# A planned kernel whose scheduler counts TensorE's turns between large and small products

## The chip, the cores and the metric

The kernel runs on one core of one Trainium2 chip. The metric is the device time of one execution in microseconds, the median of several runs. Before the change it is 1898.14 us (three runs, 1898.09 to 1899.59).

## The reference

The reference is a two-layer decoder trunk on one sequence of 1024 positions and 1024 channels, in float32. Each layer computes `x + rms_norm(mixer(rms_norm(x)))`.

- Layer 0 projects the normed input with one matrix into two groups. Group A is a gated DeltaNet of 8 heads (key and value width 128): a causal convolution of four taps and SiLU on q, k and v, then a recurrence over time, `S = exp(g) S (I - beta k k^T) + beta k v^T`, `o = S^T q`. Group B is an S5 recurrence: 64 groups of 16 channels with 64 complex states each, then GELU and a gate `y * sigmoid(y @ w_glu)`. Each group is multiplied by a SiLU gate, and both go through one output projection of 2048 by 1024.
- Layer 1 projects into four parts of 2048 channels (b, c, h, z), computes `b * conv3(c * h) * silu(z)` with a causal convolution of three taps, and projects back with a matrix of 2048 by 1024.

## The kernel before

The kernel does not issue its instructions in the order in which the code names them. Every engine call goes through a recorder (`Queue`, `Plan.record`, line 154): it notes the engine, the tiles read and written, a duration from a table (`Plan.cost`, line 170) and a priority. The priority is the place of the call in the program; inside `with nc.after(n)` (line 92) n is added, which makes the calls less urgent. When all is recorded, `Plan.order` (line 222) plays the program through: an instruction is ready when what it depends on has ended and its tiles have a buffer; each engine, when free, takes the ready instruction of lowest priority number; the time goes on by the table's duration. `Plan.emit` (line 318) then issues all instructions in the order of the planned start times, through one line, so that the whole profile stands under line 323. What the plan decides is thus the order on each of the queues (TensorE, VectorE, ScalarE, GpSimd, SyncE's DMAs); on the chip each queue runs in that order, and every instruction starts when its semaphores allow.

The precision of float32 comes from pairs. A factor is split into a high and a low part of the fp32r type (`split`, line 368: a ScalarE copy and a VectorE subtraction), and a product is three fp32r matmuls of 128x128 by 128x512: high by high, high by low, low by high. Matmuls that add into the same PSUM bank form a chain in the plan: the next is ready when the one before has ended. The small work stays in plain float32: transposes against an identity, products with 128 columns, and products on 32x32 and 64x64 tiles.

The work in order of the program:

- `setup` (line 532) loads x in 8 blocks of 128 rows, normalizes, and transposes into hh and hl (`to_hT`, tiles hTp).
- S5 runs in 8 rounds (`s5_front`, `s5_scan`, `s5_back`: tiles mbp, pk, px on TensorE, then py), between projections (`u_proj`, `z_proj`: tile mm).
- DeltaNet runs in a pipeline over heads (line 517 on): in one turn the front of head i-1, the back of head i-2, and the projections of head i, which stand under `nc.after(400)`. The front (line 1009) transposes k (ktp), multiplies k by k and q (kk), transposes v (pv) and q (qtp), and inverts a triangular matrix (`invert`, line 1118: tiles iy, it, ip, in levels of 32 and 64 with copies on VectorE and a long substitution on GpSimd). The back (line 1062) is a chain over 8 chunks (pks, pz, pS) and a transpose (po).
- `glu` (line 1175), then the first output projection (`out_proj`, line 1225): first all 8 row blocks for the lower half of the channels, then all 8 for the upper half. When the upper half of a row block is done, `finish` (line 1289) normalizes it: ScalarE squares, VectorE scales, GpSimd takes the power -1/2 (tiles orr and n1r). Then `to_B` (line 427), under `nc.after(150)`, transposes it in two groups of four (tile hTq, PSUM of the ring g, which has three banks), and ScalarE copies the result out (tile r). From block 4 on, GpSimd combines the copies (tiles Bx and r).
- Layer 1 (`layer1`, line 1355) multiplies 2x2 blocks by a scheme of seven products instead of eight (`proj2`, line 1303; products p1 to p7, shown as p). The first two need blocks 0 to 3 alone; the others need `combine` (line 469), which follows GpSimd's work on blocks 4 to 7, and sums of the weights (tiles s, wb, wa), also on GpSimd.
- The second output projection (`out_proj1`, line 1380) writes the result.

The table of durations for TensorE has, in us: fp32r with n columns n/2400 + 0.0134; a transpose n/1200 + 0.003; plain float32 with 128 stationary columns n/600 + 0.005; narrow tiles 0.03 to 0.115. A turn from one kind to another costs nothing in the plan.

Of the kernel before, what the change touches and what calls it, by code (L numbers as in the profile page):

```python
# [10 lines left out]
F32R = mybir.dt.float32r  # L11
# [48 lines left out]


class Op:
    __slots__ = ("eng", "call", "dur", "dma", "deps", "succ", "wait", "ready", "start", "tiles", "prio", "port")


class Queue:
# [7 lines left out]
class Plan:  # L74
# [4 lines left out]

    LAT = dict(PE=0.2, DVE=0.12, ACT=0.15, Pool=0.11)  # L80

    WINDOW = 3.4133

    def __init__(self, nc):
# [69 lines left out]
    def record(self, eng, call, method, a, k):  # L154
        op = Op()
        op.eng, op.call, op.deps, op.succ, op.prio = eng, (call, a, k), {}, [], len(self.ops) + self.prio
        isap = lambda x: isinstance(x, bass.AP)
        outs = [x for x in a[:1] if isap(x)] + [k[n] for n in ("out", "accum_out") if n in k]
        ins = [x for x in a[1:] if isap(x)] + [x for n, x in k.items() if n not in ("out", "accum_out") and isap(x)]
        for x in ins:  # L160
            self.touch(op, x, False)
        for x in outs:
            self.touch(op, x, True)
        op.dma = method == "dma_start"
        op.dur = self.cost(eng, method, outs, ins, a, k)
        op.port = self.port(op, ins, method)
        self.ops.append(op)


# [50 lines left out]
        return t.tag.rsplit("_", 2)[0]  # L220

    def order(self):
        from heapq import heappush, heappop
        ops = self.ops
        rings = {}
        for h in self.tiles.values():
            t = h["tile"]
            h["n"] = len(h["users"])
            if t.space != bass.MemoryType.DRAM:
                rings.setdefault(self.ring(t), []).append(h)  # L230
        for op in ops:
            op.tiles, op.wait, op.ready = [], len(op.deps), 0.0
            for j, kind in op.deps:
                ops[j].succ.append((op, kind))
        for h in self.tiles.values():
            for op in h["users"]:
                op.tiles.append(h)
                if h["tile"].space != bass.MemoryType.DRAM:
                    op.wait += 1
        idx = {op: i for i, op in enumerate(ops)}  # L240
        later = {e: [] for e in ("PE", "DVE", "ACT", "Pool", "SP")}
        now = {e: [] for e in later}
        free = {e: 0.0 for e in later}
        hw = dma = port = 0.0
        clock, edge, busy = 1.0, self.WINDOW, 0.0

        def unblock(op, t):
            op.ready = max(op.ready, t)
            op.wait -= 1
            if op.wait == 0:  # L250
                heappush(later[op.eng], (op.ready, op.prio, idx[op]))

        def grant(ring, t):
            h = ring.pop(0)
            for op in h["users"]:
                unblock(op, t)

        for op in ops:
            if op.wait == 0:
                heappush(later[op.eng], (0.0, op.prio, idx[op]))  # L260
        for key, hs in rings.items():
            for _ in range(min(self.caps.get(key, 1), len(hs))):
                grant(hs, 0.0)
        done = []
        while len(done) < len(ops):
            e = min(later, key=lambda e: free[e] if now[e] else max(free[e], later[e][0][0]) if later[e] else 1e18)
            t = free[e] if now[e] else max(free[e], later[e][0][0])
            while later[e] and later[e][0][0] <= t:
                r, p, i = heappop(later[e])
                heappush(now[e], (p, i))  # L270
            op = ops[heappop(now[e])[1]]
            op.start = t
            done.append(op)
            if op.dma:
                issue, move, late = op.dur
                if e == "Pool":
                    free[e] = t + issue
                    dma = max(dma, t + issue + 1.0) + move
                else:
                    hw = max(hw, t + 0.03) + issue  # L280
                    free[e] = hw
                    dma = max(dma, hw + 0.65) + move
                end, lat = dma + late, 0.0
            elif e == "PE":

                while t >= edge:
                    clock = 1.0 if busy > (0.5 if clock == 1.0 else 0.75) * self.WINDOW else 0.5
                    edge += self.WINDOW
                    busy = 0.0
                free[e] = end = t + op.dur / clock  # L290
                busy += min(end, edge) - t
                while end >= edge:
                    over = min(end - edge, self.WINDOW)
                    clock = 1.0 if busy > (0.5 if clock == 1.0 else 0.75) * self.WINDOW else 0.5
                    edge += self.WINDOW
                    busy = over
                lat = self.LAT[e]
            else:
                if op.port:
                    t = max(t, port)  # L300
                free[e] = end = t + op.dur
                if op.port:
                    port = end
                lat = self.LAT[e]
            for s, kind in op.succ:
                x = lat + (0.02 if s.eng == "PE" and e != "PE" else 0.045 if s.eng == "Pool" else 0.0)
                if s.eng == e and not op.dma and (kind == "WAR" or e == "PE"):
                    x = 0.0
                unblock(s, end + x)
            for h in op.tiles:  # L310
                h["n"] -= 1
                h["end"] = max(h["end"], end + lat)
                if h["n"] == 0 and h["tile"].space != bass.MemoryType.DRAM and rings[self.ring(h["tile"])]:
                    grant(rings[self.ring(h["tile"])], h["end"])
        self.time = max(free.values())
        return sorted(range(len(ops)), key=lambda i: (ops[i].start, i))
# [1214 lines left out]
```

## Time and profile before

| | us |
|---|---|
| median of three runs | 1898.14 |
| the profiled execution's own time | 1899.18 |
| its span, first to last instruction | 1897.4 |
| PE busy | 1852.5 (98%), 9733 matmul records |
| VectorE busy | 1241.2 (65%) |
| GpSimd busy | 897.7 (47%) |
| ScalarE busy | 657.6 (35%) |

PE is TensorE's matmul queue and PEld its loads of stationary operands; a plain float32 product makes two matmul records, an fp32r product or a transpose one. The products are pipelined: a row's length is longer than its distance to the next row, and the distance from start to start is what a product costs. Rows with a count (x4) join neighbours of one kind. The granted clock is a share of 2.4 GHz; 0.5 is the level of 1.2 GHz. A releaser after an arrow is what ended the wait before the row.

### The profile page before, as it was taken

Reading aid. Unit: us, or ns where it says so; the run is one execution under the profiler, and the core shown is the slowest. Engines: PE = TensorE matmul, PEld = TensorE weight load, DVE = VectorE, ACT = ScalarE, POOL = GpSimd, SP = SyncE. Lnnn points to the kernel's source line nnn. Section 1 sums busy time; section 2 is a strip of 40 time slices with the busy share of each in tenths; the row PEclk is TensorE's granted clock in tenths of the full one; section 3 lists DMA queues with packets and bytes.
Section 4 is the critical chain, followed back from the end, with each engine's and each line's share of the span. In section 5 each row is a group of like instructions: output and inputs, shape, how many; then the busy total and the mean of one; then the engine's idle time right before and its main releaser. Section 6 shows DMA issues by size and latency. Waiting matters only on the chain.

```text
span 1897.4 us, 25853 instructions
## 1 busy us (share of the span) xinstructions
PE 1852.5 (98%) x9733; PEld 1521.8 (80%) x9733; DVE 1241.2 (65%) x1966; ACT 657.6 (35%) x1373; POOL 897.7 (47%) x1003
## 2 busy tenths in 40 slices
PE   7999999999999999999999989999999999999998
PEld 5877888788888888788888757888888888888887
DVE  5957687877787777766525677667666766676131
ACT  5222223344444443534425542322232223233120
POOL 1188780433553345430001587877776777662000
PEclk9999999999999999999999989999999999999999
DMA  9445454212212223467635411232122222237130
GB/s 232 120 116 157 136 141 137 64 45 56 63 53 76 68 60 86 145 187 251 213 101 167 137 49 55 61 99 67 56 78 78 67 56 75 82 99 245 56 134 34
DMA packets 250844, 199.29 MB, mean 105 GB/s; under 512 B 12064, under 2 KB 226144, under 8 KB 250720
## 3 DMA queue, kind: packets, MB, share of 16 engines
q1 hardware_dynamic: 230112, 184.54, 32.8%
q10 hardware_dynamic: 20608, 13.12, 2.8%
q8 instruction: 76, 1.25, 0.3%
q14 instruction: 48, 0.39, 0.1%
HBM read 150.46 MB, written 42.96 MB: 102 GB/s over the span
## 4 chain that ended last, share of the span: by engine, by line
PE 86%; DVE 6%; DMA 3%; POOL 2%; issue 1%; ACT 1%; SPq 1%; ACTq 0%; POOLq 0%; DVEq 0%
PE mm L323 40%; PE p L323 31%; PE ob L323 2%; PE oa L323 2%; PE py L323 1%; PE pS L323 1%; PE kk L323 1%; PE pks L323 1%; PE iy L323 1%; DVE cm L323 1%; PE px L323 1%; PE pz L323 1%; DMA Z<-X 1%; DMA Dm<-gcd 1%; SPq L323 1%
## 5 line engine op out<-in xcount | busy, mean ns | idle before, releaser
L323 PE MATMUL mm<-hh,wl 128*128 128x512 f32 x768 | 310.9, 405 | 4.5 <-DVE wl L323 4.5
L323 PE MATMUL mm<-hh,wh 128*128 128x512 f32 x768 | 309.1, 402 | 0.4 <-ACT hh L323 0.4
L323 PE MATMUL mm<-hl,wh 128*128 128x512 f32 x768 | 308.1, 401 | 0.0
L323 PE MATMUL p<-B,ah 128*128 128x512 f32 x768 | 239.6, 393 | 4.8 <-DVE g L323 2.7
L323 PE MATMUL p<-BT,ah 128*128 128x512 f32 x768 | 240.4, 394 | 2.5 <-ACT BT L323 1.9
L323 PE MATMUL mm<-wo,yh 128*128 128x512 f32 x768 | 240.0, 393 | 0.2 <-ACT yh L323 0.2
L323 PEld LDWEIGHTS p<-B,ah 128*128 128x128 f32 x768 | 144.8, 189 | 37.3 <-DVE g L323 3.3
L323 PEld LDWEIGHTS p<-BT,ah 128*128 128x128 f32 x768 | 145.8, 190 | 34.8 <-ACT BT L323 2.3
L323 PEld LDWEIGHTS mm<-hh,wl 128*128 128x128 f32 x768 | 145.5, 189 | 30.4 <-DVE wl L323 4.9
L323 PEld LDWEIGHTS mm<-wo,yh 128*128 128x128 f32 x768 | 144.0, 188 | 31.4 <-ACT yh L323 0.6
L323 PEld LDWEIGHTS mm<-hh,wh 128*128 128x128 f32 x768 | 145.7, 190 | 26.6 <-ACT hh L323 0.8
L323 POOL TENSOR_TENSOR orr<-ot,mhalf 128x1 f32<-128x1 f32 x16 | 13.2, 822 | 325.1 <-DVE ot L323 325.0
L323 PEld LDWEIGHTS mm<-hl,wh 128*128 128x128 f32 x768 | 145.4, 189 | 26.7 <-issue 0.9
L323 PE MATMUL p<-BT,al 128*128 128x512 f32 x384 | 150.7, 393 | 4.4 <-DVE al L323 4.4
L323 PE MATMUL mm<-wo,yl 128*128 128x512 f32 x384 | 151.5, 395 | 0.4 <-DVE yl L323 0.4
L323 PE MATMUL p<-B,al 128*128 128x512 f32 x384 | 150.7, 393 | 0.2 <-DVE al L323 0.2
L323 POOL TENSOR_TENSOR inv<-L,inv 128x60 f32<-128x60 f32 (+24 forms) x248 | 93.4, 376 | 88.0 <-DVE L L323 42.6
L323 DVE SCALAR_TENSOR_TENSOR xp<-mm,cw,xp 128x512 f32<-128x512 f32 (+4 forms) x168 | 111.8, 669 | 17.6 <-ACT xp L323 8.1
L323 DVE TENSOR_TENSOR yl<-yin,yh 128x896 fp32r<-128x896 f32 (+2 forms) x70 | 51.1, 765 | 98.6 <-ACT yh L323 81.9
L323 ACT CAST ah<-wa 128x1024 fp32r<-128x1024 f32 x64 | 67.2, 1052 | 129.9 <-PE p L323 79.3
L323 DVE TENSOR_TENSOR al<-wa,ah 128x1024 fp32r<-128x1024 f32 x64 | 93.4, 1459 | 13.6 <-ACT ah L323 12.4
L323 DVE TENSOR_TENSOR wl<-ws,wh 128x1024 fp32r<-128x1024 f32 x56 | 75.6, 1350 | 35.1 <-ACT wh L323 35.0
(299 smaller groups left out, 3841.3 us busy)
## 6 DMA issues: line engine op xcount, KB each, us to landing
ws<-in_w_in SPq DMA_DIRECT2D x48, 512.0 KB, 4.3
wo<-in_w_out SPq DMA_DIRECT2D x32, 512.0 KB, 4.6
wa<-in_w_in SPq DMA_DIRECT2D x32, 512.0 KB, 4.3
wb<-in_w_in SPq DMA_DIRECT2D x32, 512.0 KB, 5.4
yin<-yd SPq DMA_DIRECT2D x32, 448.0 KB, 4.4
zzd<-zt SPq DMA_DIRECT2D x16, 512.0 KB, 3.6
y1d<-y SPq DMA_DIRECT2D x16, 512.0 KB, 3.4
yin<-y1d SPq DMA_DIRECT2D x16, 512.0 KB, 4.1
```

The costliest lines, as they stand in the source:

```text
L323: f(*a, **k)
```

## The change

`Plan.order` gets a notion of TensorE's kind. An instruction of TensorE is small when its table duration is under 0.13 us and its stationary operand isn't fp32r: all transposes, and the products on narrow tiles (mbp, pk, px, iy, it, ip, bat, gcp). The rest is large: the fp32r matmuls, and also the plain float32 products of 128 by 128 and more (kk, pks, pz, pS, py).

When TensorE is free and the most urgent ready instruction is of the other kind than the last one, the plan looks through the ready instructions in order of priority for one of the same kind. From large to small it looks 20 places beyond the most urgent, from small to large 100. If it finds one, that one runs and the most urgent goes back. If it finds none, TensorE turns, and the plan's time goes on by 0.14 us (to small) or 0.2 us (to large) before the instruction starts. No instruction is added or removed.

```diff
+    TURN, STAY = (0.2, 0.14), (20, 100)
...
+        op.small = eng == "PE" and op.dur < 0.13 and ins[0].dtype != F32R
...
+        small = False
...
             op = ops[heappop(now[e])[1]]
+            if e == "PE":
+                if op.small != small:
+                    for x in sorted(now[e]):
+                        if x[0] > op.prio + self.STAY[small]:
+                            break
+                        if ops[x[1]].small == small:
+                            heappush(now[e], (op.prio, idx[op]))
+                            now[e].remove(x)
+                            heapify(now[e])
+                            op = ops[x[1]]
+                            break
+                if op.small != small:
+                    small = op.small
+                    t += self.TURN[small]
             op.start = t
```

## Rows read from the trace of the kernel before

**Rows 1.** Busy time, share of the span and count, from the page.

```profile
PE 1852.5 (98%) x9733; PEld 1521.8 (80%) x9733; DVE 1241.2 (65%) x1966; ACT 657.6 (35%) x1373; POOL 897.7 (47%) x1003
```

**Rows 2.** Stretches: length, PE busy and count, granted clock, DMA share, GB/s.

```profile
0.00:100.00 100.00, 87.72 (x394) 1.00 0.64 172
340.00:365.00 25.00, 20.43 (x81) 0.86 0.21 56
1080.00:1123.00 43.00, 32.29 (x122) 0.88 0.17 50
1123.00:1152.00 29.00, 26.27 (x102) 0.88 0.19 55
```

**Rows 3.** TensorE in order of time: start, length, engine, line, operation, tiles, shape, count.

```profile
1013.54 0.27 PE L323 MATMUL hTq<-cst,xs 128*128 128x128 f32 x1
1013.57 0.48 PE L323 MATMUL mm<-wo,yl 128*128 128x512 f32 x1
1013.88 0.27 PE L323 MATMUL hTq<-cst,xs 128*128 128x128 f32 x1
...
1014.93 0.63 PE L323 MATMUL mm<-wo,yh 128*128 128x512 f32 x2
```

**Rows 4.** Groups of instructions by line, TensorE: the transposes hTq, busy and mean ns.

```profile
L323 PE MATMUL hTq<-cst,xs 128*128 128x128 f32 x64 | 16.3, 273 | 0.7 <-DVE xs L323 0.7
```

**Rows 5.** TensorE in order of time, the eight transposes of row block 7.

```profile
1092.81 1.10 PE L323 MATMUL hTq<-cst,xs 128*128 128x128 f32 x8 [0.69 <-DVE xs L323]
1093.66 0.48 PE L323 MATMUL p<-B,al 128*128 128x512 f32 x1
1093.97 0.62 PE L323 MATMUL p<-B,ah 128*128 128x512 f32 x2
1094.44 0.63 PE L323 MATMUL p<-B,al 128*128 128x512 f32 x2
```

**Rows 6.** TensorE in order of time, a level of the inversion.

```profile
506.95 0.39 PE L323 MATMUL mm<-hh,wl 128*128 128x512 f32 x1
507.27 0.69 PE L323 MATMUL iy<-inv,LA 32*32 32x32 f32 x32
507.89 0.50 PE L323 MATMUL mm<-hh,wh 128*128 128x512 f32 x1
508.23 0.40 PE L323 MATMUL mm<-hl,wh 128*128 128x512 f32 x1
```

**Rows 7.** TensorE in order of time, the start of a head's front.

```profile
520.50 0.60 PE L323 MATMUL kk<-kq 128*128 128x256 f32 x2
520.93 0.60 PE L323 MATMUL ktp<-cst,kq 128*128 128x128 f32 x4
```

**Rows 8.** TensorE in order of time, from the projection's end into layer 1.

```profile
1076.58 0.28 PE L323 MATMUL hTq<-cst,xs 128*128 128x128 f32 x1
...
1080.97 0.62 PE L323 MATMUL p<-B,ah 128*128 128x512 f32 x2
...
1082.34 0.28 PE L323 MATMUL hTq<-cst,xs 128*128 128x128 f32 x1
...
1085.44 0.27 PE L323 MATMUL hTq<-cst,xs 128*128 128x128 f32 x1
...
1089.09 1.19 PE L323 MATMUL p<-B,ah 128*128 128x512 f32 x4 [1.54 <-ACT ah L323]
```

**Rows 9.** The chain of waits in order of time: start, length, what.

```profile
1085.75 0.64 ACT r L323 x2
...
1111.75 4.65 PE p L323 x10
```

**Rows 10.** GpSimd in order of time.

```profile
1086.46 1.06 POOL L323 TENSOR_TENSOR Bx<-r,r 128x256 f32<-128x256 f32 x1
...
1090.95 0.55 POOL L323 TENSOR_TENSOR n1r<-n1ss,mhalf 128x1 f32<-128x1 f32 x1
```

**Rows 11.** VectorE in order of time.

```profile
1088.53 0.14 DVE L323 TENSOR_SCALAR n1ss<-n1ss 128x1 f32<-128x1 f32 x1
```

More of the change, by code (lines that the diff above doesn't have):

```diff
@@ L62 @@
 class Op:
-    __slots__ = ("eng", "call", "dur", "dma", "deps", "succ", "wait", "ready", "start", "tiles", "prio", "port")
+    __slots__ = ("eng", "call", "dur", "dma", "deps", "succ", "wait", "ready", "start", "tiles", "prio", "port", "small")
 class Queue:
@@ L222, in order @@
     def order(self):
-        from heapq import heappush, heappop
+        from heapq import heapify, heappush, heappop
         ops = self.ops
```

## The prediction

> **What bounds the kernel now.** I read the busy table first, then PE's time by stretches, then the instructions in order of time where PE's two kinds of product alternate. TensorE is busy for 98% of the span [rows 1]: of 1897.4 us only 44.9 are without a product (1897.4 - 1852.5). So a change of the order on TensorE can gain in two ways only: the same products follow each other more tightly, or one of the few holes closes. The holes are few and in known places [rows 2]. The first 100 us hold 12.3 us of idle PE (the start). From 340 to 365 us there are 4.6 us idle, and the granted clock of 0.86 means 25.0 x 0.14 x 2 = 7.0 us at the 1.2 GHz level instead of 2.4, which loses 3.5 more. From 1080 to 1123 us (the first output projection hands over to layer 1) 10.7 us are idle and 43.0 x 0.12 = 5.2 us are lost to the low level; from 1123 to 1152 us 2.7 and 3.5. The last three stretches together cost 30.2 us. All the rest is dense.
>
> **The first term, the transposes of the handover.** The plan calls small what it prices under 0.13 us and what is not fp32r: all transposes, and the products on narrow tiles. Where both kinds are ready together is the second half of the first output projection: the transposes hTq carry a priority of 150 later than their place, reach a tie with the running matmuls, and then one transpose and one matmul take turns, because each chain frees its next member only when the last has ended [rows 3]. With the rule, TensorE stays with the matmuls until they are 20 places behind the transpose, then stays with the transposes: the 4 of a group, and those of the next group, 12 places on, follow in one run. There are 64 hTq [rows 4], 8 for each of 8 row blocks.
>
> What is that worth? In rows 3, from 1013.54 to 1014.93 us, four transposes and four matmuls take 1.39 us. A matmul among its own kind takes 0.23 (from 1093.97 on, two in 0.47, [rows 5]); more exactly 0.228, as the six from 1080.97 to 1082.34 [rows 8] take 1.37. So a transpose in alternation costs (1.39 - 4 x 0.228)/4 = 0.120 us. The grouped price stands in rows 5: eight transposes and the matmul behind them take 1093.97 - 1092.81 = 1.16 us, which leaves (1.16 - 0.228)/8 = 0.117 each. Inside the group the step is 0.85/8 = 0.106. A regrouped transpose saves 0.003 us by the whole run and 0.014 by the step alone: for the 56 that alternate 0.2 to 0.8 us, and I take 0.5. The plan charges 0.34 for such a round trip; the trace has a thirtieth of it.
>
> **The second term, the narrow tiles.** Here a turn does cost. Before 32 records of iy on 32*32 tiles a matmul takes 507.27 - 506.95 = 0.32 us to its successor, and the first one behind them 508.23 - 507.89 = 0.34 [rows 6]: over the 0.228 that is 0.09 and 0.11, so a turn of 0.2 us. But such runs cannot be joined: each level of the inversion waits for VectorE's copy of the one before. And in the front of a head the small products are hundreds of places more urgent than the matmuls of the next projection, which carry +400, so neither 20 nor 100 places change the choice. What can be joined is a case like the kk that runs ahead of a head's second group of ktp [rows 7]: kk counts as large, and with 100 places of patience both ktp groups come first where PSUM allows. That is one turn in a head, at most the 0.2 us of rows 6: eight heads give 0 to 1.6, and I take 0.4, near the low end because ktp has the same 128*128 tile as the transposes of the first term.
>
> The Trainium skill (TensorEngine Tiling (Array Packing), Key Properties) says that a change of the tiling mode, and not of the tile alone, drains TensorE. Rows 3 and 6 agree with it: the 128*128 transposes turn for almost nothing, the 32*32 products do not. By that rule a boundary drawn at duration and type saves nothing on hTq and ktp, both gains above would be 0, and the sum would end 0.9 us higher than by the rows.
>
> **The third term, GpSimd behind the transposes.** Grouping moves transposes. Block 5's start at 1076.58 us and layer 1's first product at 1080.97 [rows 8]; between lie 4.39 us, of which the eight transposes take 1.0, so 15 matmuls of the projection. Fewer than 20, so the transposes now wait for all of them and run as eight at about 1080.1. The projection's own end comes earlier by 8 x 0.11 = 0.9 us. Block 6's second four, of which the last starts at 1085.44 us now, wait for layer 1's first 24 products. These begin at 1080.97 as before, since block 5's group has only changed its place before them, and take 24 x 0.228 = 5.5, so the four start at about 1086.5 and the last at 1086.8, 1.4 later than now; nothing else of layer 1 is ready before 1089.09 [rows 8]. Behind them ScalarE copies and GpSimd combines, and the chain of waits runs through just this: from block 6's last transpose to ACT r at 1085.75, then GpSimd almost without a pause up to VectorE's al and the product at 1111.75 [rows 9]. GpSimd's Bx of block 6 starts at 1086.46 [rows 10]; 1.4 us later is the delay at first sight. Against it stands that block 7's scalar orr and n1r are queued on GpSimd behind block 5's and 6's combines: n1r runs at 1090.95 [rows 10], and block 7's transposes wait for it. With block 6 late and the projection 0.9 earlier, n1r can slip ahead: VectorE has its input ready at 1088.53 + 0.14 = 1088.67 [rows 11], up to 2.3 us sooner. So the term lies between -2.3 and +1.4, with one more low-clock stretch as in 340 to 365 us, +4.9. I take 1.4 - 0.9 = +0.5: the late start, less the earlier end. If GpSimd had other work for the pause (the operand sums s and wb of the second product set), it would be 0.
>
> **The fourth term, everything else that is re-planned.** The plan adds 0.2 or 0.14 us to its own clock at each turn, so its TensorE runs later against VectorE, ScalarE, GpSimd and the DMA queue, whose instructions are sorted by these times. No instruction is added or removed on any queue. Where two evacuations or splits now stand in the other order, a product waits or stops waiting. The trace before shows no such exchange, so it is bounded by the holes: at best a stretch like 340 to 365 us closes (-8.1), at worst one more like it opens (+8.1). I take 0, as rows 2 show dense work outside these stretches.
>
> **Sum.** -0.5 - 0.4 + 0.5 + 0 = -0.4 us on the profiled execution, whose own time was 1899.18 us (span 1897.4 and 1.8 around it). That lies 1.04 over the median of 1898.14, so on the median's scale 1897.7; I predict 1897.7 us. A measurement of this kernel can tell about 0.2%, 3.8 us, from no change.
>
> **Rivals.** *A hole closes (faster).* The plan's TensorE has been too fast wherever narrow tiles turn (0.2 us, [rows 6]); with the charge its times fit better, and an evacuation or a weight split that now comes late is put in time. For it: the three stretches of 30.2 us come from order, not from bandwidth. Against it: the charge falls on hTq and ktp too, where it is wrong. Price: the stretch from 340 to 365 us, 4.6 + 3.5, gives 1897.7 - 8.1 = 1889.6; half of it 1893.6.
>
> *GpSimd's chain decides (slower).* Place: 1080 to 1123 us. If block 6's combines start after about 1087.9 (1086.46 + 1.4) and GpSimd finds nothing for the pause, each of its steps up to 1111.75 is later, and the longer hole brings another stretch at 1.2 GHz: +1.4 + 3.5 over the other terms of -0.9 gives 1902.1. It decides from the point where block 7's n1r does not come sooner than 1090.95. For it: the chain runs through this place. Against: TensorE catches up if block 7 comes sooner.
>
> *The rule doesn't bite.* Transposes find no ready neighbour, alternation stays, only the plan's clock moves: 1898.1, within the bound like the forecast.
>
> **How the numbers follow.** The forecast has 0.36 and the rule that doesn't bite 0.08, which makes 0.44 within 0.2%. A closed hole or several gets 0.33: the 30.2 us are there to be won, and any re-sorting touches them. Slower gets 0.23, by GpSimd's chain or by a new hole of the size of 8.1 us, which would be 1905.8. The forecast's own range is 1895.4 (-2.3 in the third term) to 1902.1. For 8 in 10 I go down to 1888 (the stretch from 340 to 365 us closes, and 1.6 of the others) and up to 1905, just under a new hole of full size.
>
> **What would show it.** Right: hTq in some 9 to 20 runs in place of alternation, at 0.11 to 0.12 us each; iy as before; block 6's Bx on GpSimd later than 1086.46 and block 7's n1r sooner; idle PE within 3 us of 10.7 from 1080 to 1123. The first term is wrong if TensorE's time from 1005 to 1080 us falls by over 2 us. The forecast is wrong if the idle time or the granted clock in the three stretches moves by more than 4 us in sum, or a hole opens where the kernel before had none.

## Result and the profile after

The changed kernel takes 1907.85 us (median of 6 runs, 1904.52 to 1909.49) against 1898.12 for the kernel before (6 runs beside it): a ratio of 1.0053, 95% interval 1.0040 to 1.0067. It is slower, outside the predicted range (1888 to 1905), where 1897.7 and no measurable change were forecast. Its profiled execution took 1907.63 us with a span of 1905.8, 8.4 over that of before. In the experiments below, four runs that took 2312 to 5550 us (one each of e1, e4 and e9, and one of the kernel before) count in the medians but in no ratio.

The busy table of the changed kernel has the same products in a longer span; compare [rows 1].

```profile
PE 1852.2 (97%) x9733; PEld 1519.9 (80%) x9733; DVE 1239.1 (65%) x1966; ACT 660.2 (35%) x1373; POOL 891.9 (47%) x1003
```

Stretches of the changed kernel (columns as in [rows 2]), the same four and three more, two of the S5 rounds and one of the heads:

```profile
0.00:100.00 100.00, 87.40 (x390) 1.00 0.61 167
95.00:125.00 30.00, 25.45 (x156) 0.89 0.34 94
125.00:200.00 75.00, 71.79 (x519) 1.00 0.52 142
340.00:365.00 25.00, 21.53 (x98) 1.00 0.34 72
370.00:850.00 480.00, 475.39 (x3104) 1.00 0.26 77
1080.00:1123.00 43.00, 32.99 (x133) 0.92 0.28 83
1123.00:1152.00 29.00, 24.64 (x99) 0.89 0.13 37
```

Three of them in the kernel before, which no row ahead shows:

```profile
95.00:125.00 30.00, 27.28 (x167) 0.94 0.33 95
125.00:200.00 75.00, 72.86 (x528) 1.00 0.59 156
370.00:850.00 480.00, 477.56 (x3117) 1.00 0.28 82
```

Between 95 and 125 us idle PE goes from 2.7 to 4.6 us and the granted clock from 0.94 to 0.89; more is lost to 200 us and in the heads.

Fixed windows blur, as everything behind a loss is shifted. Another measure is the start of the n-th fp32r matmul record (tiles mm, p, oa and ob in the order of the trace, the first being number 0), in us, and the change against the kernel before:

| record | about where | before | after | change |
|---|---|---|---|---|
| 300 | setup through | 93.4 | 94.2 | +0.9 |
| 400 | first S5 front | 124.8 | 129.5 | +4.8 |
| 500 | second S5 round | 160.7 | 169.3 | +8.6 |
| 1100 | first heads | 361.9 | 368.9 | +7.0 |
| 2800 | heads and GLU through | 918.8 | 928.9 | +10.1 |
| 3400 | first output projection | 1059.0 | 1069.2 | +10.2 |
| 3750 | layer 1 steady | 1166.1 | 1175.0 | +8.9 |
| 6900 | end | 1880.6 | 1889.0 | +8.4 |

This measure has a blind spot: where small products of other tiles run sooner or later than before, the n-th fp32r record shifts although no time is lost. At 500 the changed kernel has run 28 more records of py (columns as in [rows 2], tile py alone), first before, then after:

```profile
0.00:160.70 160.70, 4.89 (x36) 0.99 0.59 155
0.00:169.30 169.30, 8.44 (x64) 0.98 0.56 155
```

At 0.11 us from start to start they are 3.1 of the 8.6 us. At 1100, 2800, 3400 and 3750 the numbers of other records differ by four at most. So some 5.5 us are lost by the second S5 round, 7.0 by the first heads, and 3 more in the heads; the handover from the first output projection to layer 1, where the forecast looked, gives 1.3 back. The first and largest loss can be seen on TensorE where the first S5 front's transposes mbp stand. The kernel before, TensorE in order of time:

```profile
103.78 0.39 PE L323 MATMUL mm<-hl,wh 128*128 128x512 f32 x1
106.89 1.69 PE L323 MATMUL mbp<-cst,W 128*128 128x128 f32 x8 [2.72 <-POOL W L323]
```

The changed kernel:

```profile
102.38 0.39 PE L342 MATMUL mm<-hh,wh 128*128 128x512 f32 x1
107.32 1.97 PE L342 MATMUL mbp<-cst,W 128*128 128x128 f32 x8 [4.55 <-POOL W L342]
```

TensorE arrives 1.4 us sooner and waits for GpSimd's sum W, which ends hardly later. The last addition into W, before:

```profile
103.64 3.20 POOL L323 TENSOR_TENSOR W<-W,wt 128x1024 f32<-128x1024 f32 x1
```

and after:

```profile
103.95 3.31 POOL L342 TENSOR_TENSOR W<-W,wt 128x1024 f32<-128x1024 f32 x1
```

It ends at 106.84 and 107.26. TensorE comes sooner because it has done less: the stretches up to mbp, counting tile mm alone (third column, in brackets), have 347 matmuls before

```profile
0.00:106.80 106.80, 82.74 (x347) 1.00 0.64 173
```

and 337 after:

```profile
0.00:107.20 107.20, 79.76 (x337) 0.99 0.62 171
```

Ten matmuls, 10 x 0.228 = 2.3 us, stand behind mbp in the queue instead of ahead of it. The kernel before had run ten more by 104.17 us, so there was work to fill the wait; it stood behind mbp, and a queue runs in its order.

### The profile page after: what moved, and what is told of

The parts are those of the page before. It is cut to its first block, busy times and chain, and to the rows that moved or that the text cites. A ratio compares the mean times of both kernels' runs of the same rounds, so it can differ in the third digit from the quotient of the medians.

```text
span 1905.8 us, 25869 instructions
## 1 busy us (share of the span) xinstructions
PE 1852.2 (97%) x9733; PEld 1519.9 (80%) x9733; DVE 1239.1 (65%) x1966; ACT 660.2 (35%) x1373; POOL 891.9 (47%) x1003
## 4 chain that ended last, share of the span: by engine, by line
PE 84%; DVE 6%; POOL 2%; DMA 2%; ACT 1%; issue 1%; ACTq 0%; POOLq 0%; DVEq 0%; SPq 0%
PE mm L342 40%; PE p L342 30%; PE ob L342 2%; PE oa L342 2%; PE pks L342 1%; PE pS L342 1%; PE py L342 1%; PE kk L342 1%; DVE xp L342 1%; POOL r L342 1%; DMA Z<-X 1%; PE px L342 1%; DMA Dm<-gcd 1%; DVE LA L342 1%; PE iy L342 1%
## 5 line engine op out<-in xcount | busy, mean ns | idle before, releaser
L342 PE MATMUL p<-B,ah 128*128 128x512 f32 x768 | 239.7, 393 | 13.0 <-ACT ah L342 10.2
L342 DVE TENSOR_TENSOR al<-wa,ah 128x1024 fp32r<-128x1024 f32 x64 | 94.2, 1471 | 7.6 <-ACT ah L342 6.0
```

The source lines that it names most:

```text
L342: f(*a, **k)
```

## Experiments

The theory after the first comparison (A in the expectations) was this: the charge of 0.2 and 0.14 us is time that the plan gives to TensorE and the chip does not take. The plan's TensorE therefore runs late against the other engines, so too few matmuls stand in its queue ahead of a product that waits for another engine. The first rival (B): it is the patience, the grouping itself, that costs. All twelve kernels were timed in five rounds, in three groups of four, each beside its own runs of the kernel before (medians 1895.84, 1896.08 and 1895.55 us; its profiled execution of 1899.18 was thus a longer one). "At 500" and so on is the change in the table's measure, taken from one profiled execution each. Executions of one kernel differ too, and the granted clock with them: of the kernel before beside e9 to e12, one took 1892.19 us at 0.996 and another 1899.1 at 0.991. The profiled executions of e5, e6, e7, e8 and e10 are the slowest of their kernel, that of e12 the fastest. So a change of 2 or 3 us between two traces can be chance. The column at 500 has the blind spot told above: e2, e7 and e10 have run the same 28 records of py more, e11 has run 62 small records fewer and e4, e8 and e12 76 fewer; for the others the counts agree.

| kernel | median us | ratio, 95% interval | at 500 | at 1100 | at 2800 | at 3750 |
|---|---|---|---|---|---|---|
| after | 1907.85 | 1.0053 (1.0040 to 1.0067) | +8.6 | +7.0 | +10.1 | +8.9 |
| e1 grouping alone | 1897.77 | 1.0012 (1.0002 to 1.0022) | +0.6 | +1.4 | +0.8 | -1.0 |
| e2 charge alone | 1904.29 | 1.0047 (1.0029 to 1.0064) | +8.4 | +2.5 | +7.0 | +3.4 |
| e3 after, sum W late | 1897.18 | 1.0007 (0.9998 to 1.0016) | -3.0 | -5.0 | -1.0 | -2.1 |
| e4 before, sum W late | 1890.79 | 0.9968 (0.9955 to 0.9980) | -3.3 | -6.6 | -3.9 | -7.5 |
| e5 before, held once | 1896.76 | 1.0011 (0.9999 to 1.0023) | +8.8 | +8.7 | +6.5 | +1.9 |
| e6 charge from the gates on | 1899.75 | 1.0022 (1.0010 to 1.0035) | +0.1 | +0.3 | +5.3 | +3.6 |
| e7 narrow tiles only | 1899.21 | 1.0026 (1.0014 to 1.0039) | +9.7 | +5.2 | +8.0 | +3.4 |
| e8 grouping, sum W late | 1891.92 | 0.9986 (0.9974 to 0.9997) | -4.7 | -4.6 | -2.1 | -3.5 |
| e9 grouping without hold | 1892.82 | 0.9982 (0.9970 to 0.9994) | -3.3 | -1.7 | -2.0 | -7.2 |
| e10 half charge | 1901.91 | 1.0039 (1.0025 to 1.0053) | +10.3 | +5.9 | +7.2 | +4.9 |
| e11 before, sum W less late | 1897.85 | 1.0014 (1.0005 to 1.0023) | -7.5 | -2.0 | +1.5 | -0.7 |
| e12 no hold, sum W late | 1890.85 | 0.9977 (0.9967 to 0.9987) | -4.7 | -8.8 | -6.2 | -10.5 |

**e1 and e2: grouping or charge.**

```diff
# e1
-    TURN, STAY = (0.2, 0.14), (20, 100)
+    TURN, STAY = (0.0, 0.0), (20, 100)
# e2
+    TURN, STAY = (0.2, 0.14), (-1, -1)
```

> The changed kernel with both charges of a turn set to 0 us, the patience of 20 and 100 places kept: grouping alone. Theory A (the charges, which the chip's transposes do not take, move the plan's TensorE late, so that products that wait for another engine stand too early in its queue): the first S5 transposes mbp stand behind 347 matmuls of tile mm again, not 337, the hole before them is 2.9 us at 103.8 and not 4.7 at 102.4, the low clock there lasts 3.4 us and not 6.9; the time is 1895 to 1899 us, as before or a little under, since the handover (1080 to 1165 us) gained 1 to 2. Theory B (the grouping holds larger products back and costs in the S5 rounds and heads): 1904 to 1908 us.

> The changed kernel with no patience (the most urgent ready product always runs), the charges of 0.2 and 0.14 us kept: charge alone. Theory A: the whole loss stays, 1905 to 1911 us, with mbp behind 337 matmuls and a hole of 4.5 to 5 us at 102 us. Theory B: 1896 to 1900 us.

The charge alone costs 0.47%, nearly the whole loss; grouping alone costs 0.12%. Without the charge mbp stands behind 347 matmuls and TensorE waits 3.42 us there, with it behind 337 and 4.26: theory A, though e1 came out in the upper half of its band, slower than the kernel before and not a little faster. Grouping is not free either. The bands up to e4 were set beside 1898.12 us for the kernel before, which ran 2.3 us lower here; e2 and e3 came out just under their bands by their time and inside them by their ratio.

**e3 and e4: the plan puts mbp later.** Only the plan's price of one GpSimd instruction changes.

```diff
         PT(W, W, wt, ADD)
+        if b == 0:
+            nc.ops[-1].dur += 4.5
```

> The changed kernel; in the plan alone GpSimd's sum W of the first S5 front is priced 4.5 us longer, so that the plan puts the first mbp behind 357 matmuls and not 337; no instruction is added or removed. Theory A: the hole at 102.4 us (4.7) and its low clock (3.5 lost) close, 1899 to 1902 us. Rival C (GpSimd is what bounds the S5 start, and TensorE's wait only moves to the next products, px and py): 1904 to 1908 us, with waits of the same sum between 107 and 200 us.

> The kernel before with the same longer price of the first sum W in the plan: mbp behind 367 matmuls in place of 347. Theory A: its hole of 2.9 us at 103.8 and 1.7 us of low clock close, 1893 to 1895 us. Rival C: 1897 to 1899 us.

In e3 the changed kernel goes from 1.0053 to 1.0007, some 8.7 us for one price, and the hole is gone. TensorE in order of time, e3:

```profile
107.19 0.39 PE L342 MATMUL mm<-hh,wl 128*128 128x512 f32 x1
107.62 1.09 PE L342 MATMUL mbp<-cst,W 128*128 128x128 f32 x8
```

and its stretches:

```profile
95.00:125.00 30.00, 29.96 (x186) 1.00 0.40 108
125.00:200.00 75.00, 74.29 (x539) 1.00 0.59 158
```

GpSimd still ends W at 107.57 us, but TensorE has 357 matmuls ahead of mbp instead of 337, is never idle there and keeps the level of 2.4 GHz. Rival C falls for e3: its waits of px and py between 95 and 205 us are 0.7 us in all. The kernel before has the same flaw, smaller, and the same price makes it 0.32% faster, more than its band said: e4 is, level with e12, the fastest kernel of the study by its median. There a part of the wait did move: py waits 5.6 us in the same stretch, 2.1 before, and the gain is seen at 1100 (-6.6) and not yet at 500, where 76 small records are still to come.

**e5: a late TensorE without any turns.** In the kernel before, one transpose of the setup is priced 2 us longer in the plan.

```diff
             self.to_hT(xs, m, hT, 0, group)
+        next(o for o in reversed(nc.ops) if o.eng == "PE").dur += 2.0
```

> The kernel before, without turns or patience; in the plan alone the last transpose of the setup is priced 2 us longer, so that the plan's TensorE runs late from there and the first mbp stands behind 337 matmuls, as in the changed kernel, not 347. No instruction is added or removed. Theory A (a plan whose TensorE is late is enough, turns are not needed): the S5 start loses what the changed kernel lost there, a hole of 4.5 to 5 us at 102 us, low clock for 6.9 us and waits of py up to 200 us, 6 to 8 us by the 500th matmul; whole time 1901 to 1905 us. Rival D (the loss needs the charges in the S5 rounds themselves): under 3 us lost by the 500th matmul, 1896 to 1899 us.

TensorE in order of time, e5:

```profile
102.56 0.39 PE L323 MATMUL mm<-hh,wh 128*128 128x512 f32 x1
108.60 1.97 PE L323 MATMUL mbp<-cst,W 128*128 128x128 f32 x8 [5.64 <-POOL W L323]
```

The S5 loss is there in full, +8.7 at 1100 (+7.0 after the change), with 337 matmuls ahead of mbp; W itself ends at 108.54 us here, 1.7 later than before, which adds to the wait. So neither turns nor grouping are needed for this loss, only a plan that is 2 us late at one point. Rival D falls. The whole time missed its band: 1896.76, not 1901 to 1905, and not clear of the kernel before. The trace wins 2.2 us back by record 2800 and 4.6 in the handover; which exchange of order does it is not shown. So the S5 loss alone need not make a kernel slower in the whole. After the change, the rest of the plan did not give it back.

**e6 and e7: where the charge may fall.**

```diff
# e6
-                    t += self.TURN[small]
+                    t += self.TURN[small] if op.prio >= self.charged else 0.0
...
+            self.nc.charged = len(self.nc.ops)
             self.gates(hT)
# e7
-        op.small = eng == "PE" and op.dur < 0.13 and ins[0].dtype != F32R
+        op.small = eng == "PE" and ins[0].dtype != F32R and (ins[0].shape[0] < P or int(np.prod(ins[0].shape[1:])) < P)
```

> The changed kernel with the charges counted only from the gates on (after the S5 rounds), the patience everywhere. Theory A: the S5 start is as before (hole 2.9 us at 103.8, within 1 us at the 500th matmul), and the heads lose 3 to 5 us between the 1100th and the 2800th matmul, as with all charges; 1898 to 1902 us. Rival D: the heads' loss was carried over from the S5 rounds, 1894 to 1897 us.

> The changed kernel, but small means a product on a narrow tile (stationary operand under 128 rows or columns): the charge falls where the trace before shows a turn of 0.2 us, and not on the 128*128 transposes; hTq alternate again. If the charge only hurts where the chip does not take it (theory A): the S5 start as before (347 matmuls), the heads within 1.5 us of before, 1894 to 1899 us. If a charge of any kind in the heads makes products stand too early (0.34 charged, 0.2 taken): 3 to 5 us lost in the heads, 1899 to 1902 us.

e6 parts the two losses: the S5 rounds are as before (+0.1 at 500), and the heads lose 5.0 us between 1100 and 2800. What TensorE waits for from 370 to 920 us (total us, times, longest), e6:

```profile
PE ktp L342 <- ACT gs L342: 2.1, 4, 0.6
PE pks L342 <- DVE gs L342: 0.9, 3, 0.4
```

The kernel before, same stretch:

```profile
PE ktp L323 <- ACT gs L323: 0.6, 4, 0.2
```

ktp needs a PSUM bank that ScalarE's squares still read, pks the state that VectorE updates. These waits rise by 2.4 us; the rest of the 5.0 was not traced to single waits. e7 went against the milder half of the theory: a charge on narrow tiles only, where the trace has turns of 0.2 us [rows 6], still costs 5.2 us by 1100 and 0.26% of the whole, half of what the changed kernel loses, though its heads lost 2.8 us only. Its mbp stands behind 347 matmuls as before and waits 3.2 us, so this loss is not the ten matmuls; what it is was not taken apart. Charging 0.34 where the chip takes 0.2 costs as well.

**e8, e9 and e12: what grouping costs.** e9 sets the charges to 0 and the patience to (0, 100), e8 and e12 add the price of W from e3 to e1 and e9.

> The changed kernel with both charges at 0 (grouping alone) and in the plan GpSimd's first sum W 4.5 us longer. Theory A: the two add up, 5 us under the kernel before by the sum and 1 to 2 by the handover: 1888 to 1893 us. If the sum's gain is a matter of chance in each plan: 1893 to 1898 us.

> The changed kernel with both charges at 0 and the patience only from small to large (0 and 100 places in place of 20 and 100): transposes are grouped, but matmuls no longer hold them back. Grouping with 20 and 100 cost 0.12%. If the cost is the hold (row block 6's transposes stand behind layer 1's first 24 products, and the split ah that the next product waits for stands behind their copies on ScalarE): the wait of p for ah after hTq (4.9 us in the run of grouping alone) is under 2 us, 1892 to 1896 us, no slower than before. If grouping itself costs: 1897 to 1900 us.

> Grouping without the hold (no charges, patience 0 and 100) and the first sum W 4.5 us longer in the plan. If the hold was what grouping cost, this is as fast as the kernel before with the longer sum, which was 0.32% under the kernel before: 1888 to 1892 us. If grouping itself costs: 1892 to 1896 us.

Without the hold of 20 places grouping turns from 0.12% slower to 0.18% faster. Part of it is the handover, 4.8 us better than before between 3400 and 3750 against 1.9 in e1; part of that in turn is the granted clock of these two executions, 0.95 there in e9 and 0.90 in e1. TensorE around block 6's transposes, e1:

```profile
1086.63 1.03 PE L342 MATMUL hTq<-cst,xs 128*128 128x128 f32 x8
1092.40 1.65 PE L342 MATMUL p<-B,ah 128*128 128x512 f32 x3 [4.74 <-ACT ah L342]
```

and e9:

```profile
1079.91 1.03 PE L342 MATMUL hTq<-cst,xs 128*128 128x128 f32 x8
1080.70 0.48 PE L342 MATMUL p<-B,ah 128*128 128x512 f32 x1
...
1086.36 1.19 PE L342 MATMUL p<-B,ah 128*128 128x512 f32 x4 [1.55 <-ACT ah L342]
```

With the hold, the transposes run after layer 1's first 24 products and nothing covers what follows; without it, the products follow the transposes and cover ScalarE's copies. The rest of e9's gain is in the S5 start (-3.3 at 500), which the handover does not explain. With the price of W added, e8 and e12 gained no more than e4 alone, so the two gains did not add up here; e12's interval overlaps e4's.

**e10 and e11: half the size.** e10 halves the charges, (0.1, 0.07); e11 prices W 2.5 us longer, not 4.5, in the kernel before.

> The changed kernel with half the charges (0.1 and 0.07 us; patience of 20 and 100 kept). In the plan the first mbp stands behind 341 matmuls (337 with the full charge, 347 without). Theory A (a late TensorE in the plan costs in proportion): 2 to 5 us lost by the 500th matmul, 2 to 3 in the heads, 1899 to 1904 us. If the loss is a matter of single exchanges of order, it need not lie between: under 1898 or over 1905 us.

> The kernel before with the first sum W priced 2.5 us longer in the plan, not 4.5: mbp behind 358 matmuls (347 before, 367 with 4.5). The hole it closes was 2.9 us plus 1.7 of low clock. Theory A: most of it closes, 1891 to 1894 us, a hole of under 1 us. Otherwise 1895 to 1898 us.

Half the charge costs 0.39%, three quarters of the whole loss, and as much as the whole at 500 (+10.3, where 2 to 5 were expected): the loss isn't in proportion, as one would expect if products change places one by one. e11 closes the hole (a wait of 0.3 us is left at mbp). Its 7.5 us at 500 are in part the 62 small records that are still to come; at 1100 it is 2.0 us ahead, and it loses 3.5 by 2800, where pS and pz wait for ScalarE and VectorE. A miss for the forecast of the whole time: one price re-sorts the whole rest of the plan, and that can take back more than the hole gave.

## Why the prediction was wrong

**The step that failed** is the fourth term, "everything else that is re-planned", put at 0, with rows 2 as the reason. It holds nearly the whole loss: the charge alone (e2) is +0.47%, 8.9 us. Its bounds of 8.1 either way, one stretch like 340 to 365 us, were a little too narrow; the value of 0 was wrong, and the chance of the side (slower 0.23) was too low. The reasoning went wrong in its sign: the rival of the closing hole said that the charge would make the plan's TensorE fit better. At mbp the chip's TensorE was already early against GpSimd, so the plan's TensorE was late and not too fast there: the waits of the trace of before have 2.7 us on GpSimd's W, between 95 and 125 us, which the prediction counted as dense. Making TensorE later in the plan widens just that hole, to 4.55 us, and pricing W later closes it (e3). The heads add some 3 us by other waits.

**The first term** was right in its size. hTq come in six runs instead of alternation, of 12 and 8, not in 9 to 20, as the ring's three banks allow three groups, which the prediction had put at two. TensorE in order of time after the change:

```profile
1028.44 1.47 PE L342 MATMUL hTq<-cst,xs 128*128 128x128 f32 x12
1029.67 0.48 PE L342 MATMUL mm<-wo,yl 128*128 128x512 f32 x1
1029.98 0.63 PE L342 MATMUL mm<-wo,yh 128*128 128x512 f32 x2
```

Twelve cost 1.54 - 0.228 = 1.31 us, 0.109 each against 0.120 in alternation: 56 x 0.011 = 0.6 us, where 0.5 was said.

**The second term** was too small to test in the whole time, but the traces show its order. Grouping alone (e1) leaves the runs of ktp as they were. With the charge, in e2 as in the changed kernel, six heads have both groups in one run, one head before. This is the joining that the term counted as a gain, and it came with a longer wait for ScalarE in front of the run:

```profile
523.41 1.09 PE L342 MATMUL ktp<-cst,kq 128*128 128x128 f32 x8 [0.61 <-ACT gs L342]
```

From 370 to 920 us ktp waits 2.2 us for ScalarE after the change and 0.6 before. A level of iy enters and leaves as before (0.31 and 0.33 us after the change, [rows 6]). The rule of the Trainium skill (TensorEngine Tiling (Array Packing), Key Properties), that a change of the tiling mode drains TensorE, agrees with these two steps against 0.228 among fp32r matmuls, and with the 0.109 and 0.120 us of the transposes.

**The third term** named the right chain with the wrong size. GpSimd in order of time, after the change:

```profile
1100.73 0.73 POOL L342 TENSOR_TENSOR Bx<-r,r 128x256 f32<-128x256 f32 x1
1101.41 0.55 POOL L342 TENSOR_TENSOR n1r<-n1ss,mhalf 128x1 f32<-128x1 f32 x1
```

Less the shift of 10.2 us that this stretch inherits, block 6's Bx starts 4.1 us later than in [rows 10], not 1.4, and n1r stands at 1091.2, no sooner. On TensorE block 6's transposes came where the forecast put them: the eight start at 1095.95, the last of them at about 1086.5 less the shift, where 1086.8 was said. Why Bx is late all the same shows on ScalarE, in order of time:

```profile
1097.97 0.62 ACT L342 ACTIVATE r<-hTq,npre 128x128 f32<-128x128 f32 x2
1098.48 1.05 ACT L342 ACTIVATE xs<-xr 128x1024 f32<-128x1024 f32 x1
1099.52 1.65 ACT L342 ACTIVATE r<-hTq,npre 128x128 f32<-128x128 f32 x6
1101.01 1.09 ACT L342 CAST ah<-wa 128x1024 fp32r<-128x1024 f32 x1
```

The square of block 7 stands between the copies, and the split ah, for which layer 1's next product waits, behind them all. That wait was 1.54 us before [rows 8]; now it is 5.17:

```profile
1102.15 1.95 PE L342 MATMUL p<-B,ah 128*128 128x512 f32 x4 [5.17 <-ACT ah L342]
```

The stretch from record 3400 to 3750, before and after:

```profile
1059.00:1166.10 107.10, 93.66 (x384) 0.92 0.25 74
1069.20:1175.00 105.80, 90.22 (x379) 0.94 0.25 75
```

Idle PE rises by 2.1 us, and yet the stretch is 1.3 us shorter, as less of it ran at the low level in this execution. So the slower rival's wait did come, but it added some 2 us of idle time only, and other losses of the handover shrank by more. What grouping costs in the whole (0.12%, e1) has its share in the hold, as e9 shows.

**Open** stays which exchanges make up the 2.6 of 5.0 us in the heads (e6), the loss of e7, what e5 wins back, and the 3.5 that e11 loses in the heads; no run took these apart.

## What to carry to other kernels

In a program whose queues are ordered by a plan, a charge is not a penalty alone: it moves that engine's clock against all others, and each product that waits for another engine moves with it in the queue. Look first where the trace already shows a short wait of the bound engine with free work behind it: there the plan is early with the other engine. Time added to the bound engine made it worse here, and a later price of the other engine's instruction gained (e4: 0.32% for one number, though e11 with a smaller one gained nothing). Then time the whole, as one changed price re-sorts everything behind it. And when the order changes, measure progress at points where the same work is done.

## What was not expected of the hardware

Grouped transposes on the full tile cost TensorE 0.109 us each, and in strict alternation with fp32r matmuls 0.120: a turn between such kinds is worth 0.01 us here. GpSimd's last sum into W, 128x1024, took 3.20 to 3.38 us in every trace in which VectorE's split wl ran on into it, before for 1.0 us (wl from 102.58 to 104.64, W from 103.64), and 2.33 us in e5 and e10, where wl had ended. The plan has 2.49; how much of the wait at mbp comes from that, no run shows.
